# Four raw buffers, four weight slots and smaller groups in the first FFN pass of a hybrid attention and mLSTM layer

## The chip, the cores and the metric

The kernel runs on one core of a Trainium2 chip. The metric is the device time of one execution in microseconds (us). Five engines work side by side, each through its own instructions in order: TensorE (PE) multiplies 128-wide tiles into PSUM, VectorE (DVE) and ScalarE (ACT) do the elementwise work, GpSimd (POOL) a little more of it, and SyncE (SP) issues the DMAs. An instruction starts when those ahead of it on its engine have started and the results that it needs are there.

## What is computed

One layer of a flow-matching backbone: attention and an mLSTM scan side by side, joined by an output projection, then a SwiGLU feed-forward network (FFN), for 128 context tokens and 1024 latent tokens. What the change touches is the FFN and what runs beside its first part:

```python
def swiglu(h, w_gu, w_down):
    g, u = jnp.split(h @ w_gu, 2, axis=-1)
    return (jax.nn.silu(g) * u) @ w_down
...
    mix = jnp.concatenate([attn_o, hm], axis=-1) @ w_out
    x = x + g1 * mix
    h2 = rmsnorm(x, norm2_w) * (1 + sc2) + sh2
    x = x + g2 * swiglu(h2, w_gu, w_down)
```

D_MODEL is 1024, D_FF 2816, that is 22 pieces `f` of 128. All values are 32-bit floats.

## The kernel before

The nine token blocks of 128 are taken three at a time (CT = 384 tokens). The FFN goes over its weights twice: a first pass for the first three blocks, while the attention of the other six is still being finished, and a second pass for those six. The second pass (`weights6`, `pair6`, L1588 on) uses sums of quarter matrices, in 16-bit parts, with fewer products.

**First pass.** `gate_up` (L1476) takes one `f` after another: for the gate and the up half it loads 128 x 1024 weights and runs 24 matmuls (`products`, L1472 to L1474). Weights and activations are split in an upper part that TensorE takes at full rate and a lower part for the rest, so each product is three matmuls. `load_piece` (L157) makes the split: a DMA into a raw buffer (L173), a cast on ACT into the upper part `whi` (L174), a subtraction on DVE into the lower part `wlo` (L175, recorded as L145), and for `gate_up` a sum of magnitudes on ACT (L178, the tally, tile `jk`), from which the second pass takes its scale. Then tanh on ACT (L1490), two products on DVE (L1491, L1492, tile `tn`, which also free the PSUM banks), and the split of the result into `hl` (ACT L1495, POOL). `down` (L1499) multiplies a group of up to five `f` with 512 columns of the down weights (L1214 to L1216); each of its three results is scaled by the gate on DVE (L1203) and added to the residual (L1204).

**Buffers.** Each name in `raw_tags` and `piece_tags` is a pair of buffers. Before, one raw pair (two raw buffers) and five pairs for `whi` and `wlo` serve the first pass; a counter walks round them. The fifth pair, `iraw0`, becomes a second raw pair when the second pass begins.

**Groups.** The 22 `f` go in groups of 4, 4, 4, 5 and 5. The first three are woven with the attention of the other blocks: scores S on TensorE (L1128), maximum on DVE (L1130), exponential on ACT (L1131), upper part `ph` on ACT (L1134) and lower part `pl` on DVE (L1135), turned by DMA (L1137, L1138), times values on TensorE (`po`, L1152, L1153), rescaled by ACT L1155 and DVE L1157. The last two groups are woven with the output projection of the last three blocks (`attn_out`, L1250 to L1254) and with `features6`, which scales (ACT L1553), transposes (PE L124) and splits (L1561 to L1585) the inputs of the second pass.

**Joint of the passes.** After the last `down`, `weight_scale` (L1537) takes the largest tally, transposes it (L124), finds a power of two on one partition (DVE L200, L190 to L193, tile `pv`), and spreads it with a matmul (L204) and a copy (L205). ACT L1605 and DVE L1606 then scale and split the weights of `f` 0 (and their sums `S`, L1597 to L1600), and the second pass's matmuls (L1619 to L1621) begin.

**What sets the order.** The order of each engine's instructions is fixed when the kernel is built, by a scheduler that runs the written program through its own model of time; `weave` hands it pieces of two streams in turn. The hardware keeps that order.

Of the kernel before, what the change touches and what calls it, by code (L numbers as in the profile page):

```python
# [8 lines left out]
F32 = mybir.dt.float32  # L9
# [4 lines left out]
AF = mybir.ActivationFunctionType  # L14
# [19 lines left out]
CB = 3  # L34
NCH = NB // CB
CT = CB * P
GROUPS = [(0, 4), (4, 4), (8, 4), (12, 5), (17, 5)]
SIX = [(0, 4), (4, 4), (8, 4), (12, 4), (16, 3), (19, 3)]
T1, T2, T3, T4, B22, B11, B21 = range(7)
A11, A12, S3, S1, S2, S4, A22 = range(7)  # L40
# [2 lines left out]
NG = 3  # L43
# [6 lines left out]
def hybrid_step(ctx: ExitStack, tc: tile.TileContext, I: dict, O: dict):  # L50
    nc = tc.nc
    mm = nc.tensor.matmul
    act = nc.scalar.activation
# [12 lines left out]
    def weave(main, side, n_main, n_side):  # L66

        due = 0.0
        for units in main:
            due += n_side / n_main * (units or 1)  # L70
            while due >= 1.0:
                next(side, None)
                due -= 1.0

    def emit(gen):
        for _ in gen:
            pass

    def chain(*gens):
        for g in gens:  # L80
            for v in g:
                yield v
# [67 lines left out]
    raw_tags = ["iraw1"]  # L150
    piece_tags = ["wl", "ipair1", "ipair0", "wq", "iraw0"]
# [5 lines left out]
    def load_piece(srcs, shape, raw=None, own=None, tally=None):  # L157

        a, b = shape
        n = a * b  # L160

        def view(t):
            return t[:, :n].rearrange("p (a b) -> p a b", b=b)

        raw = raw_tile() if raw is None else raw
        if not own:
            loaded["n"] = (loaded["n"] + 1) % len(piece_tags)
            tag = piece_tags[loaded["n"]]
            at = homes.get(tag, wp)
            own = [at.tile([P, 1024], F32R, name=nm(t), tag=tag, bufs=2) for t in ("whi", "wlo")]  # L170
        hi, lo = own
        for part, ap_ in srcs:
            loaded["piece"] = dma(part(view(raw)), ap_).ins  # L173
        nc.scalar.copy(hi[:, :n], raw[:, :n])  # L174
        sub(lo[:, :n], raw[:, :n], hi[:, :n].bitcast(F32), "dve")  # L175
        if tally is not None:
            jk = ft.tile([P, D], BF16, name=nm("jk"), tag="t2", bufs=nt2[0])
            act(jk[:, :n], raw[:, :n], AF.Abs, accum_out=wsum[:, tally : tally + 1])  # L178
        return view(hi), view(lo)

    full_view = lambda v: v
# [1317 lines left out]
    def down(c, a, f0, nf, n):  # L1499
        g = gate_bc(1, c, n)  # L1500
        acts = a["act"]
        pieces = []
        for j in range(0, nf, 2):
            m = min(2, nf - j)
            rows = w_down[(f0 + j) * P : (f0 + j + m) * P, n * 512 : (n + 1) * 512].rearrange("(a p) n -> p a n", p=P)
            pieces.append(load_piece([(full_view, rows)], (m, 512)))
        yield from three_blocks(
            lambda k, i: (acts[k][0][:, i * P : (i + 1) * P], acts[k][1][:, i * P : (i + 1) * P]),
            pieces, nf, lambda i, ps: add_gated(a["x1"][i], ps, g(c * CB + i), n))
# [27 lines left out]
    def weight_scale():  # L1537

        dve.tensor_reduce(out=six[:, 7:8], in_=wsum, axis=AX.X, op=ALU.max)
        emit(power_scale(fp, ones, six[:, 7:8], six[:, 2:4]))  # L1540
        dve.tensor_tensor(out=six[:, 4:5], in0=six[:, 1:2], in1=six[:, 3:4], op=ALU.mult)
        dve.tensor_tensor(out=six[:, 6:7], in0=six[:, 4:5], in1=six[:, 4:5], op=ALU.mult)
        dve.tensor_scalar(out=six[:, 5:6], in0=six[:, 4:5], scalar1=0.5, scalar2=None, op0=ALU.mult)
# [44 lines left out]
    def weights6(f):  # L1588

        raws = []  # L1590
        for off in (0, D_FF):
            raw = raw_tile()
            dma(raw.rearrange("p (k n) -> p k n", k=KD), w_gu[f + (NF if off else 0)].rearrange("p (k n) -> p k n", k=KD))
            raws.append(raw)
        g, u = (raw.rearrange("p (a n) -> p a n", a=2) for raw in raws)
        S = sp.tile([P, 4, 512], F32, name=nm("S"), tag="S", bufs=1)
        dve.tensor_tensor(out=S[:, 1], in0=u[:, 0], in1=u[:, 1], op=ALU.add)  # L1597
        dve.tensor_tensor(out=S[:, 0], in0=u[:, 0], in1=g[:, 0], op=ALU.add)
        dve.tensor_tensor(out=S[:, 2], in0=S[:, 1], in1=g[:, 0], op=ALU.add)
        dve.tensor_tensor(out=S[:, 3], in0=S[:, 2], in1=g[:, 1], op=ALU.add)  # L1600
        ops = {}
        for names, v in (((A11, A12), g), ((S2, S4), S[:, 2:4]), ((S3, S1), S[:, 0:2]), ((A22,), u[:, 1:2])):
            n = len(names)
            t = a4p.tile([P, 2, 2, 512], F16, name=nm("A"), tag="A4", bufs=7)
            act(t[:, 0:n, 0], v, AF.Copy, scale=six[:, 2:3])  # L1605
            dve.scalar_tensor_tensor(out=t[:, 0:n, 1], in0=v, scalar=six[:, 2:3], in1=t[:, 0:n, 0], op0=ALU.mult, op1=ALU.subtract)  # L1606
            for j, name in enumerate(names):
                ops[name] = [t[:, j, part].rearrange("p (k n) -> p k n", k=4) for part in range(2)]
        return ops

    def pair6(f, Bt, acts):

        ops = weights6(f)
        a, b, c, d = (bank()[:, 0:CT] for _ in range(4))

        def product(n, ps, first):
            (wh, wl), bt = ops[PRODUCTS[n][0]], Bt[:, PRODUCTS[n][1]]
            for k in range(4):
                mm(ps, wh[:, k], bt[:, 0, k], start=first and k == 0, stop=False, skip_group_check=True)  # L1619
                mm(ps, wh[:, k], bt[:, 1, k], start=False, stop=False, skip_group_check=True)  # L1620
                mm(ps, wl[:, k], bt[:, 0, k], start=False, stop=k == 3, skip_group_check=True)  # L1621

        def u(tag, bufs=1):
            return up.tile([P, CT], F32, name=nm(tag), tag=tag, bufs=bufs)

        product(0, a, True)
        p1 = u("p1", 2)
        nc.scalar.copy(p1, a)
        yield
        product(1, b, True)  # L1630
        u2 = u("u2", 2)
        dve.tensor_tensor(out=u2, in0=b, in1=p1, op=ALU.subtract)
        yield
        product(2, d, True)
        yield
        product(3, c, True)
        u3 = u("u3")
        dve.tensor_tensor(out=u3, in0=c, in1=u2, op=ALU.add)
        c22 = u("c22")
        dve.tensor_tensor(out=c22, in0=u3, in1=d, op=ALU.subtract)  # L1640
        yield
        product(4, a, False)
        tn = up.tile([P, 2, CT], F32, name=nm("tn"), tag="tn", bufs=2)
        act(tn[:, 0], a, AF.Tanh, scale=six[:, 5:6])
        yield
        product(5, d, False)
        gb = u("gb")
        dve.tensor_tensor(out=gb, in0=d, in1=u2, op=ALU.subtract)
        act(tn[:, 1], gb, AF.Tanh, scale=six[:, 5:6])
        dve.scalar_tensor_tensor(out=tn[:, 1], in0=tn[:, 1], scalar=1.0, in1=c22, op0=ALU.add, op1=ALU.mult)  # L1650
        dve.tensor_tensor(out=tn[:, 1], in0=tn[:, 1], in1=gb, op=ALU.mult)
        yield
        product(6, c, False)
        c21 = u("c21")
        dve.tensor_tensor(out=c21, in0=c, in1=u2, op=ALU.add)
        dve.scalar_tensor_tensor(out=tn[:, 0], in0=tn[:, 0], scalar=1.0, in1=c21, op0=ALU.add, op1=ALU.mult)
        dve.tensor_tensor(out=tn[:, 0], in0=tn[:, 0], in1=a, op=ALU.mult)
        hl = new_hl(f)
        flat = tn.rearrange("p a n -> p (a n)")
        act(hl[:, 0], flat, AF.Copy, scale=six[:, 6:7])  # L1660
        dve.scalar_tensor_tensor(out=hl[:, 1], in0=flat, scalar=six[:, 6:7], in1=hl[:, 0].bitcast(F32), op0=ALU.mult, op1=ALU.subtract)
        acts.append(hl)
        yield
# [117 lines left out]
    cur, nxt = {}, {}  # L1781
    cur["x1"], nxt["x1"] = x1_first, new_x1(1)
    due = 0.0
    for _ in prefill(cur, nxt):
        due += 0.35
        while due >= 1.0:
            with tc.issue_after(cur["gate"]), tc.issue_after(loaded["gate"]), tc.issue_after(loaded["hm"]), tc.issue_after(loaded["pe"]):
                next(att, None)
            due -= 1.0

    hlp = es_f.enter_context(tc.tile_pool(name="hlp", bufs=1, reuse_waits="tile"))

    def groups(c, a, lst):
        for f0, nf in lst:
            yield from gate_up(a, f0, nf)
            yield from down(c, a, f0, nf, 0)
            yield from down(c, a, f0, nf, 1)
# [14 lines left out]
    with tc.issue_after(loaded["gate"]):  # L1812
        for _ in range(4):
# [10 lines left out]
    firsts = []  # L1824
    feats = chain(*[features6(nxt, 1, i, Bt, firsts) for i in range(CB)],
                  attn_out(far, o2, g_d[0, 1], lambda i: mixing(a4p, "A4", 7), o_d[CB:]), *[features6(far, 2, i, Bt, firsts) for i in range(CB)])
    main = groups(0, cur, GROUPS[NG:])
    weave(main, feats, 18 * sum(nf for _, nf in GROUPS[NG:]), 42)
    emit(feats)
    weight_scale()  # L1830
    es_f.close()
    es_ps.close()
    del psum["mm1"], psum["po"]
# [4 lines left out]
    nt2[0] = 4  # L1838
    ft = ctx.enter_context(tc.tile_pool(name="ft6", bufs=1, reuse_waits="tile"))
    fp = ctx.enter_context(tc.tile_pool(name="fp6", bufs=1, reuse_waits="tile"))  # L1840
    raw_tags.append(piece_tags.pop())
    x6 = nxt["x1"] + far["x1"]
    gs6 = row_pair(g_d[1, 1])
    done6 = finish(0, cur)
# [67 lines left out]
```

## Time and profile before

| | us |
|---|---|
| median of 3 runs (1538.3 to 1539.11) | 1538.46 |
| the profiled execution | 1538.01 |
| its span | 1536.2 |
| first pass, first L1472 to last down matmul | 651.97 to 1024.2 |
| first matmul of the second pass | 1028.40 |

Mean granted clock of TensorE 0.97. Times in the trace count from the start of the span; some 1.8 us of the execution lie outside it. A row of the timeline gives start, length, engine, line, operation, result and operands, and in brackets how long the engine stood idle before it and what ended that.

### The profile page before, as it was taken

To read this page: it belongs to the slowest core of one execution; us is meant where nothing else is said; L and a number is where in the kernel's file an instruction comes from. 1 tells how busy PE (TensorE), PEld (TensorE's weight loads), DVE (VectorE), ACT (ScalarE), POOL (GpSimd) and SP (SyncE) were. 2 spreads that over 40 slices of the span, in tenths; PEclk is the share of its full clock that TensorE was granted. 3 is DMA by queue.
4 is the path that set the end of the run, shared out by engine and by line. 5 is a ranking of instruction groups with operands and counts; after the bars stand their busy time and mean duration, and the time that the engine had idled before them with its cause. 6 is when DMAs were issued, how large, how long until landed. Compare 5 with 4: busy or idle time off the path is not lost.

```text
span 1536.2 us, 22786 instructions
## 1 busy us (share of the span) xinstructions
PE 1434.6 (93%) x8281; PEld 1071.1 (70%) x8281; DVE 1126.6 (73%) x2272; ACT 810.7 (53%) x1524; POOL 222.4 (14%) x310
## 2 busy tenths in 40 slices
PE   6889899899899889999999899989999999999995
PEld 3635567676677657888989787965766667676763
DVE  4978557685777778646787766879878696886857
ACT  4855476676766745552866752844334141523233
POOL 0122332132323344510001010000000000000000
PEclk9799999999999999999999999999999999999997
DMA  9475245565449756564778733444222040412112
GB/s 371 155 227 186 68 90 96 72 150 78 81 102 158 197 187 170 145 206 138 212 177 193 185 117 117 143 132 153 81 72 94 28 137 1 138 49 76 35 35 82
DMA packets 255318, 197.02 MB, mean 128 GB/s; under 512 B 167974, under 2 KB 209142, under 8 KB 255206
## 3 DMA queue, kind: packets, MB, share of 16 engines
q1 hardware_dynamic: 252638, 191.13, 45.9%
q10 hardware_dynamic: 2440, 4.05, 1.2%
q8 instruction: 65, 1.06, 0.3%
q0 software_dynamic: 128, 0.39, 0.1%
q14 instruction: 47, 0.39, 0.1%
HBM read 143.94 MB, written 13.26 MB: 102 GB/s over the span
## 4 chain that ended last, share of the span: by engine, by line
PE 53%; DVE 4%; DMA 4%; ACT 4%; issue 1%; POOL 1%; SPq 0%; ACTq 0%; POOLq 0%
PE mm L1621 7%; PE mm L1619 7%; PE mm L1620 7%; PE mm L1687 4%; PE mm L1688 4%; PE mm L1689 4%; PE mm L1472 3%; PE mm L1474 3%; PE mm L1473 3%; PE mm L1214 2%; PE mm L1216 2%; PE mm L1215 2%; PE mm L1250 2%; DMA raw<-in_w_gu_dram 2%; PE mm L1252 2%; PE mm L1254 1%
## 5 line engine op out<-in xcount | busy, mean ns | idle before, releaser
L1619 PE MATMUL mm<-Bt,A 128*128 128x384 f16 x616 | 200.2, 328 | 1.6 <-ACT A L1605 1.6
L1620 PE MATMUL mm<-Bt,A 128*128 128x384 f16 x616 | 201.6, 327 | 0.0
L1621 PE MATMUL mm<-Bt,A 128*128 128x384 f16 x616 | 197.2, 327 | 2.4 <-DVE A L1606 2.4
L174 ACT CAST whi<-raw 128x1024 fp32r<-128x1024 f32 (+1 forms) x102 | 103.3, 1014 | 132.5 <-DMA raw<-in_w_down_dram 49.0
L145 DVE TENSOR_TENSOR wlo<-raw,whi 128x1024 fp32r<-128x1024 f32 (+1 forms) x102 | 120.7, 1183 | 53.8 <-ACT whi L174 49.0
L1135 DVE SCALAR_TENSOR_TENSOR pl<-pr,st,ph 128x1152 f16<-128x1152 f32 (+1 forms) x72 | 95.7, 1329 | 48.8 <-ACT ph L1134 45.1
L1472 PE MATMUL mm<-aTh,whi 128*128 128x384 f32 x352 | 121.7, 346 | 8.8 <-ACT ol L1155 3.1
L1474 PE MATMUL mm<-aTh,wlo 128*128 128x384 f32 x352 | 120.9, 344 | 0.8 <-DVE wlo L145 0.8
L1473 PE MATMUL mm<-aTl,whi 128*128 128x384 f32 x352 | 120.9, 343 | 0.0
L1130 DVE TENSOR_REDUCE st<-S 128x1 f32<-128x1152 f32 (+1 forms) x72 | 88.9, 1235 | 21.7 <-PE S L1128 21.2
L1131 ACT ACTIVATE pr<-S,st 128x1152 f32<-128x1152 f32 (+1 forms) x72 | 81.5, 1132 | 40.2 <-DVE st L1130 39.7
L1134 ACT ACTIVATE ph<-pr,st 128x1152 f16<-128x1152 f32 (+1 forms) x72 | 84.0, 1167 | 32.4 <-DVE st L1133 11.7
L1128 PE MATMUL S<-kst,qT 128*128 128x384 f32 (+1 forms) x400 | 89.6, 357 | 7.1 <-ACT pr L1131 7.1
L525 PE MATMUL wi<-headw,hT 128*128 128x384 f16 x288 | 94.7, 329 | 1.6 <-ACT th L815 1.4
L526 PE MATMUL wi<-headw,hT 128*128 128x384 f16 x288 | 94.6, 328 | 0.0
L527 PE MATMUL wi<-headw,hT 128*128 128x384 f16 x288 | 94.5, 328 | 0.0
L1605 ACT ACTIVATE A<-S,six 128x1024 f16<-128x1024 f32 x44 | 49.9, 1146 | 80.8 <-PE mm L1621 58.0
L1619 PEld LDWEIGHTS <-A 128*128 128x128 f16 x616 | 60.3, 98 | 44.5 <-issue 3.8
L1621 PEld LDWEIGHTS <-A 128*128 128x128 f16 x616 | 60.4, 98 | 43.2 <-DVE A L1606 3.1
L1203 DVE TENSOR_TENSOR t<-mm,hmr 128x512 f32<-128x512 f32 x84 | 54.4, 684 | 48.3 <-PE mm L1689 33.3
L1620 PEld LDWEIGHTS <-A 128*128 128x128 f16 x616 | 60.4, 98 | 39.2 <-issue 0.5
L1128 PEld LDWEIGHTS S<-kst,qT 128*128 128x128 f32 x400 | 71.0, 194 | 10.7 <-ACT pr L1131 8.4
(456 smaller groups left out, 3694.3 us busy)
## 6 DMA issues: line engine op xcount, KB each, us to landing
raw<-in_w_gu_dram SPq DMA_DIRECT2D x88, 512.0 KB
raw<-in_w_down_dram SPq DMA_DIRECT2D x40, 512.0 KB
a<-in_w_ada_dram SPq DMA_DIRECT2D x24, 512.0 KB
iraw<-in_w_in_dram SPq DMA_DIRECT2D x32, 256.0 KB
x<-in_x_sample_dram SPq DMA_DIRECT2D x11, 512.0 KB
raw<-in_w_out_dram SPq DMA_DIRECT2D x10, 512.0 KB
aw<-in_w_ada_dram SPq DMA_DIRECT2D x8, 512.0 KB
aw<-in_w_ada_dram SPq DMA_DIRECT2D x16, 256.0 KB
```

The costliest lines, as they stand in the source:

```text
L145: (dve if eng == "dve" else pool).tensor_tensor(out=out, in0=full, in1=hi, op=ALU.subtract)
L174: nc.scalar.copy(hi[:, :n], raw[:, :n])
L525: mm(ps[:, :n], ah, wh[:, k % 2, c0 : c0 + n], start=(k == 0), stop=False)
L526: mm(ps[:, :n], ah, wl[:, k % 2, c0 : c0 + n], start=False, stop=False)
L1128: mm(S[:, n, 0:w], qT[:, h, :], kst[kv][:, t, c0 + n * w : c0 + (n + 1) * w], start=(t == 0), stop=(t == 1))
L1135: dve.scalar_tensor_tensor(out=plv, in0=prv, scalar=st[:, 3:4], in1=phv, op0=ALU.mult, op1=ALU.subtract)
L1472: mm(ps, wh[:, k, :], th[:, k, :], start=(k == 0), stop=False)
L1473: mm(ps, wh[:, k, :], tl[:, k, :], start=False, stop=False)
L1474: mm(ps, wl[:, k, :], th[:, k, :], start=False, stop=(k == KD - 1))
L1619: mm(ps, wh[:, k], bt[:, 0, k], start=first and k == 0, stop=False, skip_group_check=True)
L1620: mm(ps, wh[:, k], bt[:, 1, k], start=False, stop=False, skip_group_check=True)
L1621: mm(ps, wl[:, k], bt[:, 0, k], start=False, stop=k == 3, skip_group_check=True)
```

## The change

1. The second raw pair is joined before the first pass: four raw buffers and four weight slots there, instead of two and five.
2. The groups of the first pass are 4, 4, 4, 4, 3 and 3, as those of the second pass are. That is one more group: six more scaled additions (L1203 and L1204, twelve rows on DVE) and four more loads of gate rows. Matmuls, weight loads and casts keep their number.
3. The tally reads the upper part of the weights instead of the raw buffer. (A magnitude then lacks its low bits; it only serves to choose a power of two.)
4. The last group's second `down` is written behind `features6`; its first step, `weight_scale`, `weights6(0)`, and the rest of it follow one another, so that the second pass's first weights can be made ready behind the last down pieces.

```diff
-GROUPS = [(0, 4), (4, 4), (8, 4), (12, 5), (17, 5)]
+GROUPS = [(0, 4), (4, 4), (8, 4), (12, 4), (16, 3), (19, 3)]
...
-            act(jk[:, :n], raw[:, :n], AF.Abs, accum_out=wsum[:, tally : tally + 1])
+            act(jk[:, :n], hi[:, :n].bitcast(F32), AF.Abs, accum_out=wsum[:, tally : tally + 1])
...
-        ops = weights6(f)
+        ops = weights6(f) if f > 0 else first_ops
...
+    raw_tags.append(piece_tags.pop())
     hlp = es_f.enter_context(tc.tile_pool(name="hlp", bufs=1, reuse_waits="tile"))
...
-    main = groups(0, cur, GROUPS[NG:])
-    weave(main, feats, 18 * sum(nf for _, nf in GROUPS[NG:]), 42)
+    main = chain(groups(0, cur, GROUPS[NG:-1]), gate_up(cur, *GROUPS[-1]), down(0, cur, *GROUPS[-1], 0))
+    weave(main, feats, 18 * sum(nf for _, nf in GROUPS[NG:-1]) + 15 * GROUPS[-1][1], 42)
     emit(feats)
+    main = down(0, cur, *GROUPS[-1], 1)
+    next(main)
     weight_scale()
+    first_ops = weights6(0)
+    emit(main)
...
-    raw_tags.append(piece_tags.pop())
     x6 = nxt["x1"] + far["x1"]
```

How the instructions move, at three places. Names carry the numbers of the tiles.

**SP, before the first pass and at its beginning.** raw_1581 and raw_1585 are the gate and up weights of `f` 0, raw_1593 and raw_1597 those of `f` 1. Before, at 575.9 us and at the beginning of the pass:

```order
L173 DMA raw_1581_7888<-in_w_gu_dram 128x1024
L1234 DMA gl_1414_7100<-g_d_81 128x512
L1234 DMA gl_1415_7102<-g_d_81 128x512
L173 DMA raw_1585_7920<-in_w_gu_dram 128x1024
...
L1138 DMA_TRANSPOSE plT_1547_7710<-pl_1563_7778 128x9x128
L1192 DMA gx_1631_8196<-g_d_81 128x512
L1314 DMA x1_d2_90<-t2_1577_7877 128x512
L173 DMA raw_1593_7961<-in_w_gu_dram 128x1024
L173 DMA raw_1597_7993<-in_w_gu_dram 128x1024
```

And after:

```order
L173 DMA raw_1593_7961<-in_w_gu_dram 128x1024
L1234 DMA gl_1414_7100<-g_d_81 128x512
L1234 DMA gl_1415_7102<-g_d_81 128x512
L173 DMA raw_1597_7993<-in_w_gu_dram 128x1024
...
L1138 DMA_TRANSPOSE plT_1547_7710<-pl_1563_7778 128x9x128
L1188 DMA gl_1630_8194<-g_d_81 128x512
L1314 DMA x1_d2_90<-t2_1572_7835 128x512
L173 DMA raw_1581_7888<-in_w_gu_dram 128x1024
L173 DMA raw_1585_7920<-in_w_gu_dram 128x1024
L173 DMA raw_1624_8153<-in_w_gu_dram 128x1024
```

The loads of `f` 0 and of `f` 1 have changed places; TensorE still takes `f` 0 first.

**PE and ACT, at the transposes of the third token block.** t2_2183 (before) and t2_2189 (after) are the scaled inputs that L124 transposes; mm_2173 and mm_2183 are products of `gate_up`. Before, on PE and then on ACT:

```order
L1472 MATMUL mm_2173_10949<-aTh_1483_7374,whi_2179_10985 128x384
L124 MATMUL mm_2184_11021<-ident_91,t2_2183_11019 128x128 x4
L1473 MATMUL mm_2173_10949<-aTl_1484_7375,whi_2179_10985 128x384
...
L174 CAST whi_2179_10985<-raw_2178_10984 128x1024
L178 ACTIVATE jk_2181_10990,wsum_7083<-raw_2178_10984 128x1024
L1553 ACTIVATE t2_2183_11019<-x1_1710_8552,ry_2119_10626 128x512
```

And after, on PE and then on ACT:

```order
L1474 MATMUL mm_2183_10958<-aTh_1483_7374,wlo_2193_11007 128x384
L124 MATMUL mm_2190_10996<-ident_91,t2_2189_10994 128x128 x4
L124 MATMUL mm_2196_11039<-ident_91,t2_2195_11037 128x128 x4
L1472 MATMUL mm_2199_11055<-aTh_1483_7374,whi_2202_11058 128x384
...
L174 CAST whi_2219_11174<-raw_2218_11173 128x1024
L178 ACTIVATE jk_2187_10965,wsum_7083<-whi_2185_10960 128x1024
L1553 ACTIVATE t2_2189_10994<-x1_1710_8552,ry_2109_10581 128x512
L178 ACTIVATE jk_2194_11011,wsum_7083<-whi_2192_11006 128x1024
L1553 ACTIVATE t2_2195_11037<-x1_1710_8552,ry_2109_10581 128x512
```

The transposes stand behind the last matmul of a piece now, not within one, and ahead of their inputs on ACT stands the cast of whi_2219, which goes into the slot of whi_2192 and so waits for that same last matmul of mm_2183.

**DVE, at the end of the pass.** mm_2258 is the bank of the nine down matmuls that now stand ahead of L204 on PE; S_2252 are sums for the second pass. Before:

```order
L1203 TENSOR_TENSOR t2_2235_11287<-mm_2233_11253,gl_2219_11211 128x512
L200 TENSOR_REDUCE pv_2237_11293<-mm_2236_11291 1x1
L1204 TENSOR_TENSOR x1a_6529<-x1a_6529,t2_2235_11287 128x512
L190 TENSOR_SCALAR pv_2237_11293<-pv_2237_11293 1x1
L191 TENSOR_SCALAR pv_2237_11293<-pv_2237_11293 1x1
L192 TENSOR_SCALAR pv_2237_11293<-pv_2237_11293 1x1
L193 TENSOR_SCALAR pv_2237_11293<-pv_2237_11293 1x1
L205 COPY six_7082<-mm_2238_11299 128x2
```

And after, first some ten rows ahead, then from the transposed tally on:

```order
L1597 TENSOR_TENSOR S_2252_11309<-raw_2251_11307 128x512
...
L1491 SCALAR_TENSOR_TENSOR tn_2222_11205<-tn_2222_11205,mm_2213_11138 128x384
...
L200 TENSOR_REDUCE pv_2248_11293<-mm_2247_11291 1x1
L1204 TENSOR_TENSOR x1a_6529<-x1a_6529,t2_2236_11261 128x512
...
L1203 TENSOR_TENSOR t2_2260_11352<-mm_2258_11332,gl_2238_11267 128x512
L1204 TENSOR_TENSOR x1a_6529<-x1a_6529,t2_2257_11329 128x512
L191 TENSOR_SCALAR pv_2248_11293<-pv_2248_11293 1x1
L1204 TENSOR_TENSOR x1a_6529<-x1a_6529,t2_2260_11352 128x512
L192 TENSOR_SCALAR pv_2248_11293<-pv_2248_11293 1x1
L193 TENSOR_SCALAR pv_2248_11293<-pv_2248_11293 1x1
L205 COPY six_7082<-mm_2249_11299 128x2
```

The sums S stand ahead of the last products of `gate_up`, and the scale's small rows stand among scalings and additions.

## The prediction

> **What bounds the kernel now.** TensorE is busy for 93% of the span (the page's first line), so only stretches in which it stands still or runs slowly can give time back. The first view is busy time by stretch, over the first FFN pass (651.97 to 1024.2) and its edges: stretch in us, its length, then busy us of PE, PEld, DVE, ACT, POOL, the granted clock, DMA share and GB/s. The second lists what TensorE waited for from 650 to 1036: total us, times, longest.
>
> ```profile
> 650.00:672.00 22.00, 18.94 (x104) 17.72 (x103) 7.69 (x11) 10.66 (x18) 4.56 (x3) 0.92 0.76 195
> 672.00:858.00 186.00, 185.04 (x1009) 167.98 (x1008) 138.09 (x201) 113.49 (x162) 14.44 (x11) 1.00 0.68 179
> 858.00:895.00 37.00, 30.12 (x178) 28.28 (x178) 23.35 (x37) 27.45 (x44) 2.03 (x2) 0.95 0.63 170
> 895.00:966.00 71.00, 67.25 (x328) 58.88 (x326) 44.74 (x80) 30.98 (x49) 5.07 (x3) 0.98 0.41 129
> 966.00:1022.00 56.00, 56.00 (x303) 52.31 (x303) 43.20 (x62) 35.07 (x55) 5.96 (x5) 1.00 0.41 133
> 1022.00:1036.00 14.00, 7.99 (x35) 4.34 (x34) 11.45 (x31) 8.01 (x11) 0.00 (x0) 0.76 0.45 151
> ```
>
> ```profile
> PE mm L1472 <- ACT ol L1155: 3.1, 1, 3.1
> PE mm L1472 <- ACT whi L174: 3.1, 1, 3.1
> PE mm L1472 <- DVE tn L1492: 2.4, 1, 2.4
> PE mm L1621 <- DVE A L1606: 2.4, 1, 2.4
> PE mm L124 <- ACT t L1553: 2.2, 1, 2.2
> PE mm L204 <- DVE pv L193: 2.0, 1, 2.0
> PE mm L1619 <- ACT A L1605: 1.6, 1, 1.6
> PE po L1153 <- DMA plT<-pl: 1.1, 1, 1.1
> PE mm L1250 <- DVE t L1203: 0.9, 1, 0.9
> PE mm L1474 <- DVE wlo L145: 0.8, 1, 0.8
> ```
>
> These are single waits, 20 us in all. 672 to 858 and 966 to 1022 have next to none, so a change of the first pass can win at four places only. Waits also cost clock: where they are dense the granted clock falls (22 x 0.08 = 1.8 us of clock missing, 37 x 0.05 = 1.9, 14 x 0.24 = 3.4), and matmuls of one shape start 0.32 us apart instead of 0.18:
>
> ```profile
> 652.15 0.34 PE L1473 MATMUL mm<-aTl,whi 128*128 128x384 f32 x1
> 652.33 0.34 PE L1474 MATMUL mm<-aTh,wlo 128*128 128x384 f32 x1
> ...
> 963.76 0.52 PE L1473 MATMUL mm<-aTl,whi 128*128 128x384 f32 x1
> 964.08 0.52 PE L1474 MATMUL mm<-aTh,wlo 128*128 128x384 f32 x1
> ```
>
> So a wait of 2 us or more costs its length and about 1.6 us of slow clock behind it (the slow rows at 963 stand behind the 2.2 us wait of L124). The Trainium skill, "TensorE: Matmul & The Clock Gate", section "What's actually happening", has the array fall to half clock only after an idle window of about 3.4 us. By that rule only the new wait at the entry would be followed by a slow clock, and the sum below would be 6.1 us smaller (1.3 + 3 x 1.6). The trace differs (half clock behind 2.2 us), and I go by the trace.
>
> **The change, part by part.** Matmuls and weight bytes stay the same. Losses now: entry 3.1 + 1.6 = 4.7; 858 to 895, 6.9 + 1.7 = 8.6; 895 to 966, 3.75 + 1.6 = 5.3; 1022 to 1036, 6.0 + 2.2 (the part of the 3.4 in which it worked) = 8.2.
>
> Entry of the pass. With four raw buffers f 0's two loads fall on the newly joined pair, which still holds the last piece of the output projection; they wait for its last matmuls, and stand behind plT and three short DMAs on SP. Those of f 1 and one of f 3 go early in their place, but TensorE still starts with f 0.
>
> ```profile
> 651.06 1.08 PE L1254 MATMUL mm<-whi,mx 128*128 128x512 f32 x4
> 653.96 2.00 SPq L1138 DMA_TRANSPOSE plT<-pl  x1
> 658.46 1.37 SPq L173 DMA_DIRECT2D raw<-in_w_gu_dram  x2
> 663.80 1.04 ACT L174 CAST whi<-raw 128x1024 fp32r<-128x1024 f32 x1 [3.81 <-DMA raw<-in_w_gu_dram]
> 666.17 0.33 SPq L173 DMA_DIRECT2D raw<-in_w_gu_dram  x1
> 669.44 1.05 ACT L174 CAST whi<-raw 128x1024 fp32r<-128x1024 f32 x1 [0.66 <-DMA raw<-in_w_gu_dram]
> ```
>
> plT can start at about 651.9 and takes 2.0, the short DMAs about 1.3: loads leave at 655.2. A pair took 5.3 us to its cast (658.46 to 663.80), a single load 3.3 (666.17 to 669.44); I take 5, since these are a pair. With the cast (1.05) TensorE starts f 0 at 661.2 instead of 652.0. Of the 9.2 us, 2.0 are filled by 18 po matmuls that moved ahead; the third matmul then waits 1.0 more for the low half; slow clock 1.6. Loss 9.8, **5.1 more** than now (1.3 to 6.2, by the two load times and with or without the clock).
>
> Middle (858 to 895). The casts come earlier, tn L1491 stands ahead of the softmax rows on DVE, and the 3.1 and 2.4 us waits go (the first L1472 after 869 reads the bank that L1491 frees; the page names another). Late next is the last head's softmax:
>
> ```profile
> L1130 DVE TENSOR_REDUCE st<-S 128x1 f32<-128x1152 f32 (+1 forms) x72 | 88.9, 1235 | 21.7 <-PE S L1128 21.2
> L1131 ACT ACTIVATE pr<-S,st 128x1152 f32<-128x1152 f32 (+1 forms) x72 | 81.5, 1132 | 40.2 <-DVE st L1130 39.7
> L1134 ACT ACTIVATE ph<-pr,st 128x1152 f16<-128x1152 f32 (+1 forms) x72 | 84.0, 1167 | 32.4 <-DVE st L1133 11.7 <-issue 8.9 <-DMA phT<-ph 4.3
> 876.89 1.85 SPq L1137 DMA_TRANSPOSE phT<-ph  x1
> 880.85 0.28 PE L1152 MATMUL po<-phT,vs 128*128 128x256 f16 x1 [0.20 <-DMA phT<-ph]
> ```
>
> From its last S matmul to po it needs 1.24 + 1.13 + 1.17 + 3.96 (876.89 to 880.85) = 7.5, and about 2.2 in the queues of ACT and DVE; TensorE has 27 matmuls at 0.18 and 16 of po, 6.5 us. It waits 3.2, then 0.8 for plT, and 1.4 for phT of the head before; with 1.3 of clock 6.7 instead of 8.6: **1.9 gained** (0 to 5). The 0.8 us wait of L1474 goes too: **0.8 gained** (0 to 0.8).
>
> The transposes of features6. Four weight slots instead of five make the cast of a new piece wait for TensorE's last matmul of the piece four before. ACT works in order, and the L1553 rows that TensorE's next instruction (L124) reads now stand right behind such a cast. ACT's durations:
>
> ```profile
> 959.59 0.49 ACT L1490 ACTIVATE tn<-mm 128x384 f32<-128x384 f32 x1 [3.53 <-PE mm L1474]
> 960.32 1.05 ACT L178 ACTIVATE jk<-raw 128x1024 bf16<-128x1024 f32 x1
> 961.36 0.71 ACT L1553 ACTIVATE t<-x,ry 128x512 f32<-128x512 f32 x1
> 982.26 1.05 ACT L174 CAST whi<-raw 128x1024 fp32r<-128x1024 f32 x1
> ```
>
> For the third token block TensorE ends mm_2183, and ACT only then does cast, tally and L1553: 1.05 + 1.05 + 0.7 = 2.8 idle; then tally and L1553 again less four transposes, 1.05 + 0.7 - 0.7 = 1.0. With the clock **5.4 lost** (3.0 to 6.5) in a stretch that has no wait now. For the first block tanh, cast, L1553 and then tally, L1553 give 2.1 + 1.0 + 1.6 = 4.7, and 1.0 goes at the joins of the output projection, 5.7 against 5.3: **0.4 lost** (2 lost to 1 gained).
>
> Sums S of pass 2. L1597 now stands on DVE ahead of tn_2222, and its load follows the last low half of a raw buffer: 3.3 to 5 us in which DVE holds back L1491 and L1492. TensorE has work for most of it: **1.0 lost** (0 to 3).
>
> End of the pass. Nine down matmuls go ahead of the scale's matmul L204 and nine behind.
>
> ```profile
> 1024.45 0.68 DVE L1203 TENSOR_TENSOR t<-mm,gl 128x512 f32<-128x512 f32 x1
> 1027.19 1.15 ACT L1605 ACTIVATE A<-raw,six 128x1024 f16<-128x1024 f32 x1
> 1030.33 1.28 DVE L1606 SCALAR_TENSOR_TENSOR A<-raw,six,A 128x1024 f16<-128x1024 f32 x1
> ```
>
> But DVE's rows of the scale stand among ten adds of 0.6 (L1203, L1204). The first nine wait for three L1203 (1.1 idle); the ten adds and five small rows, 6.9, against 2.9 of matmuls and that 1.1 leave 2.9; behind L204 come 0.8 + 1.15 + 1.28 against nine matmuls and two of pass 2, 2.4: 0.9. The clock (1.6), and p1 behind three L1435 of 1.0, about 1.0. 7.5 instead of 8.2: **0.7 gained** (1.5 lost to 4 gained).
>
> At nothing: twelve more adds (12 x 0.6 = 7 us of DVE, beside matmuls; uncovered only at the end, counted there), four gate DMAs, and the tally, which keeps its length. It no longer holds the raw buffer, but the low half's subtraction does.
>
> Sum: 5.1 - 1.9 - 0.8 + 5.4 + 0.4 + 1.0 - 0.7 = **8.5 slower**: 1538.0 (profiled run; span 1536.2) becomes 1546.5, and from the median 1538.46, 0.45 above it, 1546.9.
>
> **The rivals.** *Weights ahead everywhere (faster).* If from 672 on the pass ran like 966 to 1022, with no wait, it would win 1.0 + 8.6 + 5.3 = 14.9 and 0.7 at the end, less 5.1: 1528. It decides at the casts: if ACT has them done before TensorE's last matmul of the slot, L1553 is never late. For it speaks that 49 us of ACT's waits are for raw loads; against it that they cost TensorE little, and that the order sets cast before L1553. The Trainium skill, "Perfetto Trace Analysis", section "Optimization Strategy", reads repeated gaps as too few buffers; by that rule this rival wins. The gaps quoted above are single, with different releasers. *Cancelled.* If the clock stays up behind the new waits other than the entry's (1.3 + 3 x 1.6 = 6.1: each is cut in two by four transposes or nine matmuls, which may keep it up), and the pair of loads lands in 3.3 us as the single one did (1.7), 1546.9 - 6.1 - 1.7 = 1539.1. Against it stands the slow clock behind 2.2 us. The rule of the Trainium skill on the clock, above, leads here too. *The entry and the end at their worst:* 1546.9 + 1.1 + 1.1 + 2.2 + 2.0 + 3 = 1556.
>
> **How the numbers follow.** Forecast 0.62 (1541.5 to 1553), cancel 0.15, weights ahead 0.15, worst 0.08. Two runs differ by about 0.2% without any change, 3.1 us, so 1535.4 to 1541.5 is the same. Slower 0.62 + 0.08 = 0.70, same 0.15, faster 0.15. The range, 1534 to 1553, leaves out most of the faster rival and of the worst.
>
> **What would show it.** Right: an idle of 6 us or more before the first L1472 of the pass, released by whi L174; L124 waiting twice for L1553 in the stretch before the end; a wait of L204 for pv of 2 us or more; 858 to 895 still with idle released by phT or plT. Wrong: f 0 starting right behind the output projection, L124 without waits, or L204 covered by the nine matmuls.

## The result, and the profile after

| | before | after |
|---|---|---|
| median, us (lowest to highest, 5 runs each) | 1538.46 (1536.93 to 1541.89) | 1551.47 (1548.4 to 1552.94) |
| the profiled execution; its span | 1538.01; 1536.2 | 1551.47; 1549.7 |
| mean granted clock | 0.97 | 0.97 |

The ratio, worked out from all runs, is 1.0072, 95% interval 1.0053 to 1.0091: **11.1 us slower** (8.2 to 14.0); the two medians alone differ by 13.0. The forecast was 1546.9 (1534 to 1553), slower; the median lies 4.6 us above it, inside the range. The first view of after is busy time by stretch, as in the prediction: stretch in us, its length, busy us of PE, PEld, DVE, ACT, POOL, granted clock, DMA share and GB/s. The second is what TensorE waited for from 645 to 1050: total, times, longest.

```profile
650.00:672.00 22.00, 16.36 (x81) 13.79 (x79) 7.37 (x10) 11.04 (x17) 2.56 (x2) 0.84 0.75 231
672.00:858.00 186.00, 185.78 (x1018) 169.29 (x1017) 133.09 (x195) 110.74 (x158) 14.49 (x12) 1.00 0.68 178
858.00:895.00 37.00, 33.55 (x199) 30.96 (x197) 24.87 (x42) 28.82 (x46) 2.01 (x2) 0.95 0.67 173
895.00:966.00 71.00, 64.70 (x313) 56.79 (x313) 50.01 (x84) 36.34 (x59) 4.11 (x3) 0.96 0.43 137
966.00:1022.00 56.00, 51.52 (x270) 48.22 (x269) 44.01 (x67) 31.13 (x48) 4.37 (x4) 0.96 0.36 113
```

```profile
PE mm L124 <- ACT t L1553: 7.0, 4, 2.8
PE mm L204 <- DVE pv L193: 4.3, 1, 4.3
PE po L1153 <- DMA plT<-pl: 3.2, 2, 2.7
PE po L1152 <- DMA phT<-ph: 2.9, 2, 2.3
PE mm L1214 <- DVE t L1203: 2.8, 2, 1.8
PE mm L1472 <- ACT whi L174: 1.7, 1, 1.7
```

The stretch 966 to 1022, which had no wait before, now has 4.5 us of idle and a clock of 0.96; 895 to 966 loses 6.3 us of idle instead of 3.75; 858 to 895 wins (3.45 idle for 6.9). L124 waits four times for L1553, where it waited once for 2.2 us. The rows of the timeline (start, length, engine, line, operation, operands, in brackets the idle time before and its releaser) put the new waits at the entry, at the transposes of the first and third block, and at the scale:

```profile
656.51 0.29 PE L1153 MATMUL po<-plT,vs 128*128 128x256 f16 x1 [2.71 <-DMA plT<-pl]
661.93 0.44 PE L1472 MATMUL mm<-aTh,whi 128*128 128x384 f32 x1 [1.74 <-ACT whi L174]
...
961.22 1.11 PE L124 MATMUL mm<-ident,t 128*128 128x128 f32 x4 [0.99 <-ACT t L1553]
...
1002.57 0.66 PE L124 MATMUL mm<-ident,t 128*128 128x128 f32 x4 [2.80 <-ACT t L1553]
1004.22 0.66 PE L124 MATMUL mm<-ident,t 128*128 128x128 f32 x4 [1.00 <-ACT t L1553]
...
1039.30 0.58 PE L204 MATMUL mm<-pv,ones 1*128 1x2 f32 x2 [4.34 <-DVE pv L193]
```

**How the loss is counted.** At full clock TensorE's matmuls start at fixed steps, read from the traces: 0.1755 us for L1472 to L1474, 0.228 for L1214 to L1216 and L1250 to L1254, 0.163 for L1619 to L1621, 0.109 for po, 0.103 for L124. For each kernel I took the time since one matmul that all have (the first L1250 of the last output projection ahead of the pass) and subtracted the steps of all matmuls issued since. What is left is idle and slow clock together. It leaves out what varied ahead of the pass. The table gives the loss in us by stretches of this work, each column ending where its head says (0 to 24 the entry; 206 to 230 the middle; 279 to 303 the transposes of the first block; 303 to 339 those of the others; 339 to 363 the end of the pass; then pass 2), for all kernels of this study, and behind it the timed ratio to the kernel before with its interval (for the change, from its own comparison; for the others from 6 to 12 runs against 18 to 27 of the kernel before). Each row of losses is one traced execution.

```
                 0-24 -206 -230 -279 -303 -339 -363 -448   sum  ratio
before            5.0  2.1  9.3  2.9  4.0 -0.2  8.6  4.8  36.5
after             9.6  1.0  5.5  4.3  6.4  6.7  9.3  5.9  48.8  1.0072 [1.0053, 1.0091]
e1_shift          1.7  1.0  5.9  4.3  5.2  6.7  8.3  4.8  37.9  1.0024 [1.0008, 1.0040]
e2_join_late      0.2  2.7  9.4  5.0  7.1  6.5  8.7  4.8  44.3  1.0047 [1.0031, 1.0062]
e3_join_only     10.2  1.0  6.2  1.1  3.5  0.3  6.8  4.7  33.7  0.9974 [0.9955, 0.9993]
e4_groups_only    2.0  5.6  9.2  8.3  2.5  5.0  9.6  4.8  46.9  1.0063 [1.0041, 1.0085]
e5_join_shift     0.7  1.3  6.8  0.8  4.9 -0.1  6.8  4.8  25.9  0.9941 [0.9916, 0.9965]
e6_five_groups    1.6  1.0  6.0  2.9  1.7  0.4  4.6  5.4  23.5  0.9923 [0.9895, 0.9951]
e7_place          9.5  1.0  5.4  3.7  8.8  1.6  9.4  4.8  44.1  1.0050 [1.0032, 1.0069]
e8_own_junk      10.1  1.2  2.3  6.3  5.4  2.7  8.5  4.8  41.3  1.0028 [1.0015, 1.0042]
e9_five_one_four  0.9  1.1  5.9  2.6 12.8  1.3  2.5  5.5  32.6  0.9979 [0.9964, 0.9995]
e10_five_junk     0.9  1.2  2.3  2.7  1.6  1.2  5.6  5.6  21.2  0.9893 [0.9868, 0.9918]
e11_five_tally    0.9  1.1  5.7  1.2  6.8  0.2  6.9  4.8  27.5  0.9945 [0.9924, 0.9965]
e12_scale_early   1.9  1.0  5.4  2.6  1.6  0.4  1.7  6.1  20.8  0.9899 [0.9875, 0.9924]
```

Where the order of the matmuls differs, the same amount of work is not the same matmul, so a stretch is good to about 1 us; whether the clock falls behind a wait can move one by 1.4 us more (e3 and e5 at 279 to 303; last section). The sums agree with the ratios: the change loses 12.3 us more than before by the count and 11.1 by the ratio, and the other kernels lie within 2.5 us.

### The profile page after: what moved, and what is told of

Same layout as the page of the kernel before. It is cut to its first block, busy times and chain, and to the rows that moved or that the text cites. A ratio compares the mean times of both kernels' runs of the same rounds, so it can differ in the third digit from the quotient of the medians.

```text
span 1549.7 us, 22841 instructions
## 1 busy us (share of the span) xinstructions
PE 1436.4 (93%) x8281; PEld 1070.8 (69%) x8281; DVE 1134.0 (73%) x2284; ACT 810.9 (52%) x1524; POOL 219.0 (14%) x310
## 4 chain that ended last, share of the span: by engine, by line
PE 55%; DVE 5%; DMA 3%; ACT 2%; issue 1%; POOL 1%; SPq 0%; ACTq 0%; DVEq 0%; POOLq 0%
PE mm L1619 6%; PE mm L1621 6%; PE mm L1620 6%; PE mm L1472 4%; PE mm L1474 4%; PE mm L1473 4%; PE mm L1687 4%; PE mm L1688 4%; PE mm L1689 4%; PE mm L1250 2%; PE mm L1214 2%; PE mm L1215 2%; PE mm L1216 2%; PE mm L1252 2%; PE mm L1254 1%; PE S L1128 1%
## 5 line engine op out<-in xcount | busy, mean ns | idle before, releaser
L1619 PE MATMUL mm<-Bt,A 128*128 128x384 f16 x616 | 199.7, 327 | 0.7 <-DVE u L1638 0.7
L1621 PE MATMUL mm<-Bt,A 128*128 128x384 f16 x616 | 198.0, 327 | 0.0
L174 ACT CAST whi<-raw 128x1024 fp32r<-128x1024 f32 x102 | 103.0, 1014 | 131.0 <-PE mm L1215 37.9
L145 DVE TENSOR_TENSOR wlo<-raw,whi 128x1024 fp32r<-128x1024 f32 x102 | 121.9, 1196 | 43.2 <-ACT whi L174 39.2
L1472 PE MATMUL mm<-aTh,whi 128*128 128x384 f32 x352 | 122.2, 347 | 2.3 <-ACT whi L174 1.7
L1474 PE MATMUL mm<-aTh,wlo 128*128 128x384 f32 x352 | 120.7, 343 | 0.6 <-DVE wlo L145 0.6
L1134 ACT ACTIVATE ph<-pr,st 128x1152 f16<-128x1152 f32 (+1 forms) x72 | 84.1, 1168 | 33.2 <-DVE st L1133 11.4
L1619 PEld LDWEIGHTS <-A 128*128 128x128 f16 x616 | 60.4, 98 | 43.0 <-issue 3.6
L1621 PEld LDWEIGHTS <-A 128*128 128x128 f16 x616 | 60.4, 98 | 40.0 <-issue 0.3
L1203 DVE TENSOR_TENSOR t<-mm,hmr 128x512 f32<-128x512 f32 x84 | 55.0, 685 | 45.2 <-PE mm L1689 33.6
L1128 PEld LDWEIGHTS S<-kst,qT 128*128 128x128 f32 x400 | 70.2, 192 | 12.9 <-ACT pr L1131 10.6
```

The source lines that it names most:

```text
L145: (dve if eng == "dve" else pool).tensor_tensor(out=out, in0=full, in1=hi, op=ALU.subtract)
L1128: mm(S[:, n, 0:w], qT[:, h, :], kst[kv][:, t, c0 + n * w : c0 + (n + 1) * w], start=(t == 0), stop=(t == 1))
L1472: mm(ps, wh[:, k, :], th[:, k, :], start=(k == 0), stop=False)
L1474: mm(ps, wl[:, k, :], th[:, k, :], start=False, stop=(k == KD - 1))
```

## The experiments

**Which part loses.** My theory at first was the prediction's: the early join of the raw pair costs at the entry and at the transposes, where casts wait for one of four weight slots. The rival: the smaller groups cost. Four kernels.

e1_shift is the changed kernel with the buffer counter set back:

```diff
     raw_tags.append(piece_tags.pop())
+    loaded["raw"] = -1
```

> The changed kernel, but the count of the raw buffers is set back at the join, so that the two loads of f 0 fall on the old pair and those of f 1 on the new one. Theory (f 0 waits for the buffer that the output projection still holds): f 0 starts right behind the output projection again, the wait shrinks to one of about 3 us at f 1, the entry loses 5 us instead of 9.7, 1547 in all. Rival (the loads are late because they stand on SP behind the transposes plT and the short DMAs, whatever buffer they use): TensorE still waits 6 us or more of work before f 0, 1551.

e2_join_late is the changed kernel with the join where it was:

```diff
-    raw_tags.append(piece_tags.pop())
     hlp = es_f.enter_context(tc.tile_pool(name="hlp", bufs=1, reuse_waits="tile"))
...
+    raw_tags.append(piece_tags.pop())
     x6 = nxt["x1"] + far["x1"]
```

> The changed kernel with the fourth raw pair taken from the weight slots only at the start of pass 2, as before (five slots and two raw buffers in pass 1). Theory (four slots make the casts stand ahead of L1553, and the new pair delays f 0): the entry gives back 4.5 us, the waits of L124 for L1553 (4.6 us idle with clock, third block) go, the middle loses its 3.8 again; 1541 to 1543. Rival (what is lost behind 895 comes from the groups of at most four, which put one more down phase with its adds and waits among the features): only the entry comes back and the middle is lost, so 1550 to 1551, with L124 still waiting for L1553 before the last group.

e3_join_only moves this one line the other way, in the kernel before.

> The kernel before with nothing but the early join: four raw buffers and four weight slots in pass 1, groups, tally and first weights as before. Theory: entry +4.5, middle -3.8 and -1.3 around it, the waits of L124 for L1553 in the features of the second chunk +5 to +7; 1543 to 1546. Rival (groups): entry +4.5 and middle -5.1 cancel, no new wait of L124; 1538.

e4_groups_only is the kernel before with the change's `GROUPS`.

> The kernel before with nothing but groups of at most four (six groups instead of five). Theory: one more down phase costs its waits only, +1 to +3; 1540 to 1541, L124 without waits of 2 us in the second chunk. Rival (groups are the cause of what is lost behind 895): +8 or more, 1547, with L124 waiting for L1553.

**Measured.** e1 settles the entry: with f 0 on the old pair its loss falls from 9.6 to 1.7 us (I had expected 5), and 0.5% of the time comes back. The buffer delayed f 0, not the place of the loads on SP. For the rest the rival won. The groups alone cost 0.63% (9.7 us, 6.3 to 13.1); the join alone **gains** 0.26% (4.0 us, 1.1 to 6.9), although it loses 5.2 us at the entry. The parts do not simply add: 9.7 less 4.0 is 5.7, and the change loses 11.1. Some of the difference lies at the entry: without the join, e2 and e4 lose only 0.2 and 2.0 there, where the kernel before loses 5.0, and the join's delay of f 0 undoes that. What else makes it up no run separates. The waits of TensorE in e3 from 645 to 1050 show f 0 late and L124 with a single wait, with four weight slots:

```profile
PE mm L1472 <- ACT whi L174: 3.5, 1, 3.5
PE po L1153 <- DMA plT<-pl: 2.9, 2, 2.3
PE po L1152 <- ACT whi L174: 2.2, 1, 2.2
PE mm L204 <- DVE pv L193: 1.9, 1, 1.9
PE mm L1472 <- DVE F L1563: 1.7, 1, 1.7
...
PE mm L124 <- ACT t L1553: 1.3, 1, 1.3
```

and those of e2, with five slots, show the four waits of L124 again. Here are ACT's rows ahead of the third block's transposes, first of the change, then of e2:

```profile
999.81 1.04 ACT L174 CAST whi<-raw 128x1024 fp32r<-128x1024 f32 x1 [2.68 <-PE mm L1474]
1000.76 1.05 ACT L178 ACTIVATE jk<-whi 128x1024 bf16<-128x1024 f32 x1
...
1001.81 0.71 ACT L1553 ACTIVATE t<-x,ry 128x512 f32<-128x512 f32 x1
```

```profile
999.61 1.04 ACT L174 CAST whi<-raw 128x1024 fp32r<-128x1024 f32 x1 [3.37 <-DMA raw<-in_w_gu_dram]
1000.56 1.05 ACT L178 ACTIVATE jk<-whi 128x1024 bf16<-128x1024 f32 x1
...
1001.61 0.71 ACT L1553 ACTIVATE t<-x,ry 128x512 f32<-128x512 f32 x1
```

Both have the cast, the tally and L1553 in this order, and the cast begins at the same time: in the change because TensorE has left the slot, in e2 because the load is there. With either number of slots L1553 comes 2.5 to 2.8 us too late for TensorE. What both share is the groups.

e4 without any other edit does not wait at L124 but all over the second half; its waits from 885 on:

```profile
PE mm L204 <- DVE pv L193: 4.3, 1, 4.3
PE mm L1472 <- DVE F L1563: 3.3, 1, 3.3
PE mm L1472 <- DVE tn L1492: 2.8, 1, 2.8
PE mm L1619 <- ACT A L1605: 2.5, 2, 1.9
PE mm L1472 <- DVE ry L141: 1.7, 1, 1.7
PE mm L1250 <- DVE t L1203: 1.3, 1, 1.3
```

Most releasers are on DVE. My own expectation for e4 (1 to 3 us) missed; the rival's size came true, but not its sign, L124 waiting for L1553.

**How the groups lose.** With groups of 4, 3 and 3 a down phase ends 48 matmuls ahead of the third block's transposes. New theory A: L1553 and the tally write into the three `t` buffers that the adds of that down phase still hold, so they come behind L1204. Theory B: the prediction's. e5 and e6 test the sum of it all: the best use of the join, without and with the other edits but without the groups. e5_join_shift is e3 with e1's line.

> The kernel before with the early join and the count of the raw buffers set back at it (the loads of f 0 on the old pair); groups, tally and first weights as before. Theory (the join gains once f 0 is not delayed, the groups alone lose): the first two matmul groups of the pass lose about 2 us instead of the 10 of the join alone, the rest as in the join alone; against the kernel before a ratio of 0.992 to 0.995. Rival (the loss at the entry was already hidden in the timed runs, which put the join alone at 0.997): 0.997, no better than the join alone.

e6_five_groups is e1 with the `GROUPS` of before.

> The changed kernel with the raw count set back at the join and the groups of before (two of five at the end); so it differs from e1_shift in the groups alone. Theory (groups): 8 to 10 us less than e1_shift, whose ratio was 1.0024, so 0.996 to 0.998; no wait of L124 for L1553 over 1.5 us. Rival (the tally and the first weights share the loss, or the groups cost only without the join): within 3 us of e1_shift, 1.001 to 1.003.

e7_place is the changed kernel with 44 for 42:

```diff
-    weave(main, feats, 18 * sum(nf for _, nf in GROUPS[NG:-1]) + 15 * GROUPS[-1][1], 42)
+    weave(main, feats, 18 * sum(nf for _, nf in GROUPS[NG:-1]) + 15 * GROUPS[-1][1], 44)
```

> The changed kernel with one number of the weave changed, 44 for 42 units of side work, so that the transposes of the third token block no longer stand as eight in a row 48 matmuls behind a down phase; groups and buffers as in the change. Theory A (place: L1553 comes late where it stands behind the adds L1204 of a down phase, whose t buffers it needs, with a tally before it): the waits of L124 for L1553 shrink from 7.0 us to 3 or less, 4 to 7 us faster than the changed kernel, a ratio of 1.003 to 1.005. Theory B (slots, as predicted: L1553 stands behind casts that wait for one of four slots): the waits stay near 7 us, 1.007.

e8_own_junk is the changed kernel with

```diff
-            jk = ft.tile([P, D], BF16, name=nm("jk"), tag="t2", bufs=nt2[0])
-            act(jk[:, :n], hi[:, :n].bitcast(F32), AF.Abs, accum_out=wsum[:, tally : tally + 1])
+            jk = ft.tile([P, D], mybir.dt.float8e4, name=nm("jk"), tag="jk", bufs=1)
+            act(jk[:, :n], hi[:, :n].bitcast(F32), AF.Abs, accum_out=wsum[:, tally : tally + 1], saturate=False)
```

> The changed kernel, but what the tally L178 writes and nobody reads goes to a buffer of its own (one byte an element, for want of room) instead of one of the three t buffers that L1203 and L1553 use. TensorE's order around the transposes stays. Theory A (t buffers: tally and L1553 wait for L1204): the longest wait of L124 for L1553 falls from 2.8 to 1 us or less, the four together to 2 to 3 us, 4 to 6 us faster than the changed kernel, 1.003 to 1.005. Theory B (casts that wait for a slot): tally and L1553 stay behind the casts, 2.8 us as before, 1.007.

**Measured.** e5 is 0.6% faster than before, as expected, and e6 0.8%, more than expected. e6 differs from e1 in the `GROUPS` line alone (from which the pace of the last weave also follows): 0.9923 against 1.0024, 15.5 us. By the table they come from 279 to 303 (5.2 to 1.7), 303 to 339 (6.7 to 0.4) and the end (8.3 to 4.6). So the groups are the loss, with the join (e1, e6) as without it (before, e4).

By time e8 is 6.8 us better than the change (1.0028), a little more than theory A expected, and it bears theory A out at the third block: 303 to 339 falls from 6.7 to 2.7 us. ACT's rows there, in which L1553 now stands ahead of the cast that waits for the slot:

```profile
997.36 1.05 ACT L178 ACTIVATE jk<-whi 128x1024 fp8e4<-128x1024 f32 x1
...
998.40 0.72 ACT L1553 ACTIVATE t<-x,ry 128x512 f32<-128x512 f32 x1
1000.27 1.04 ACT L174 CAST whi<-raw 128x1024 fp32r<-128x1024 f32 x1 [1.15 <-PE mm L1473]
...
1001.57 0.71 ACT L1553 ACTIVATE t<-x,ry 128x512 f32<-128x512 f32 x1
```

The first L1553 now starts where the first add ends (998.30), and the first of L124's two waits is gone. The second L1553 still stands behind the cast, and 1.5 us of wait are left. In the change itself the two reasons end within 0.7 us of each other: the adds at 1000.05, the cast, which delays the tally to 1000.76, a little later. Only e8 parts them. But the longest wait of L124 did not fall to 1 us as I expected: at the first block it rose to 3.4. There L1553 waits for the norm `ry` on DVE, which begins with the last add of the output projection. First DVE's two rows of the change, the add and the end of the norm, then ACT's row of e8:

```profile
951.50 0.68 DVE L1204 TENSOR_TENSOR x<-x,t 128x512 f32<-128x512 f32 x1
...
958.11 0.16 DVE L141 SCALAR_TENSOR_TENSOR ry<-rt,ry 128x3 f32<-128x3 f32 x1
```

```profile
961.60 1.95 ACT L1553 ACTIVATE t<-x,ry 128x512 f32<-128x512 f32 x3 [0.26 <-DVE ry L141]
```

From the add to the end of the norm 6.8 us pass. Between the last matmul of the output projection and these transposes the change has 48 matmuls of gate and up (48 x 0.1755 = 8.4 us); the kernel before has 45 of down and 24 of gate and up (45 x 0.228 + 24 x 0.1755 = 14.5 us). The groups took this cover away. In the change itself the norm ends at 958.27 and L1553 starts at 958.80, behind a tanh and a cast, so by these rows I estimate that the norm explains 1.7 of the 2.2 us that L124 waits there; no run takes the norm alone out. I had not expected e8's gain in the middle (5.5 to 2.3): with the tallies elsewhere on ACT, the last head's upper part L1134 starts 3.3 us earlier in e8 (second row) than in the change (first row), although e8 came to the pass 2.0 us later, and TensorE no longer waits for phT there.

```profile
880.11 1.26 ACT L1134 ACTIVATE ph<-pr,st 128x1152 f16<-128x1152 f32 x1 [0.52 <-ACT pr L1131]
```

```profile
876.85 1.25 ACT L1134 ACTIVATE ph<-pr,st 128x1152 f16<-128x1152 f32 x1
```

e7 moved the wait rather than removing it: 303 to 339 falls from 6.7 to 1.6, and the first block's wait grows to 5.0 us, so L124 still waits 6.4 us, which is near what theory B expected. Its interval (1.0032 to 1.0069) reaches from theory A's range nearly to theory B's 1.007; by time it decides nothing.

**Number or place, and what is left to win.** e9_five_one_four is e1 with another cut of the same number of groups:

```diff
-GROUPS = [(0, 4), (4, 4), (8, 4), (12, 4), (16, 3), (19, 3)]
+GROUPS = [(0, 4), (4, 4), (8, 4), (12, 5), (17, 1), (18, 4)]
```

> e1_shift with the last ten f cut into groups of 5, 1 and 4 in place of 4, 3 and 3: the number of groups is the change's, but the first down phase behind the features stands where groups of five put it, and no transposes stand right behind a down phase. Theory (place: 4, 3, 3 put the output projection, the transposes and the down phases so that TensorE comes to the transposes before the norm and the adds are done): within 4 us of e6_five_groups, 0.993 to 0.996. Rival (number: each group more costs its adds, gates and small pieces wherever it stands): as e1_shift, 1.000 to 1.003.

e10_five_junk is e6 with e8's edit.

> e6_five_groups, and what the tally writes gets a buffer of its own, as in e8_own_junk. Theory (the t buffers hold L1553 back behind the adds): the one wait of L124 for L1553 left in e6 (1.4 us) goes, with its neighbours 1 to 3 us; 0.990 to 0.992. Rival (with groups of five the t buffers are free in time): no change, 0.992 to 0.993.

e11_five_tally is e5 with the tally from the high half.

> e5_join_shift and the tally from the high half: e6_five_groups without the early first weights. Theory (as in the prediction, the tally gives nothing): as e5_join_shift, 0.993 to 0.995, and the early first weights then make the difference to e6 (0.9923), if there is one. Rival (raw buffers that come free a tally earlier bring loads and casts forward): 0.992 or less, as e6.

e12_scale_early is e6 with

```diff
     emit(feats)
+    weight_scale()
     main = down(0, cur, *GROUPS[-1], 1)
     next(main)
-    weight_scale()
     first_ops = weights6(0)
```

> e6_five_groups with the scale of the weights worked out one step earlier, ahead of the last down phase's second half instead of behind its first nine matmuls: the scale's matmul L204 then stands behind 33 matmuls where it stood behind 2. Theory (L204 waits for rows that DVE works off between adds, and more matmuls ahead of it cover them): the wait of 2.4 us for pv falls below 0.5, 2 to 4 us less than e6, 0.990 to 0.991. Rival (DVE is the limit: sums S and A come no earlier, the wait moves to the first matmuls of pass 2): 0.992 to 0.993.

**Measured.** e9 fell between the two expectations (0.9979). By the table it is within 2.1 us of e6 up to 279 and from 303 on, and loses 11 us more from 279 to 303, where L124 waits 2.7 us and this row stands: TensorE has nothing to do while the only `hl` of the group of one is made.

```profile
973.32 0.79 PE L1214 MATMUL mm<-whi,hl 128*128 128x512 f32 x1 [4.34 <-ACT hl L1495]
```

So six groups need not cost what 4, 3, 3 costs, which speaks for the place; but every cut brings waits of its own, and a six-group kernel without them was not found. e10 and e12 came out as fast as expected or faster: **0.9893 and 0.9899**, 16.5 (12.6 to 20.3) and 15.5 us (11.7 to 19.2) faster than the kernel before. Against e6 their intervals overlap; by the count they gain 2.3 and 2.7 us. In e12 the stretch 339 to 363 falls from 4.6 to 1.7, and L204 waits no more. Its four largest waits from 645 to 1050 are:

```profile
PE po L1152 <- DMA phT<-ph: 2.4, 1, 2.4
PE mm L1214 <- DVE t L1203: 1.9, 2, 1.1
PE mm L124 <- ACT t L1553: 1.4, 1, 1.4
PE mm L1472 <- DVE tn L1491: 0.9, 2, 0.6
```

e10's gain is not at L124, as I expected, which still waits 1.4: the table has it in the middle (6.0 to 2.3), as in e8. e11 equals e5 (0.9945 and 0.9941): no gain of the tally from the high half shows with four raw buffers. From e11 to e6 the early first weights gain 0.2% by the medians of the ratios, with overlapping intervals, and 4.0 us by the count. e10's and e12's edits were not run together.

## Why the prediction was right, and where it was not

By its own terms, forecast and then measured from the table (after less before):

- **Entry**: +5.1, measured +4.6 (a loss of 9.6 where 9.8 was forecast). Right in mechanism, by e1 and e3 (10.2 with the join alone), and f 0 starts 9.1 us behind the output projection for the 9.2 forecast. But the idle came in pieces (0.55 and 2.71 ahead of po, 1.74 ahead of the first L1472, 0.64 ahead of L1474), not as the 6 us in one piece that was to be the sign, and it is 5.6 us where 8.2 were forecast; slow clock is 4.0 where 1.6 were. That the two errors cancel is luck.
- **The wait of L1474** (24 to 206): -0.8, measured -1.1.
- **Middle**: -1.9, measured -3.8. Right in kind: the casts come earlier, and phT is late next, for 2.3 us. e3 has it (6.2), e2 without the join does not (9.4). The term was too small by half: the waits are 3.5 us (0.60, 2.34 and 0.52) for the 5.4 forecast, and the wait for phT of the head before is not there.
- **First block and joins**: +0.4, measured +3.8 (230 to 303: 10.7 against 6.9). The two waits of L124 are as forecast, 2.19 and 0.99 us for 2.1 and 1.0. Too small were the joins of the output projection, 3.1 us of waits (0.96 of L1250, 1.83 of L1214 for t, 0.32 of L1250) for the 1.0 forecast, and the slow clock behind L124. The norm, which the matmuls of a down phase covered before, is not in the step.
- **Third block**: +5.4, measured +6.9, and 2.8 and 1.0 us idle to the tenth as forecast. **This step failed in its reason.** "Four weight slots instead of five make the cast of a new piece wait" is true of the change's trace, yet with four slots and the old groups (e3) the stretch loses 0.3, and with five slots and the new groups (e2) 6.5. The row of cast, tally and L1553 was read rightly from the order; it stands where it does because of the groups.
- **Sums S of pass 2**: +1.0, measured nothing. DVE did stand 3.54 us for their load (to 1020.03), as forecast, but TensorE has no wait over 0.1 us from 1004.22 to 1032.63. The +1.1 of the column of pass 2 comes later: L1619 waits 0.51 and 0.22 us for `u` (1072 and 1086), which no term names.
- **End**: -0.7, measured +0.7. L204 waited 4.3 us instead of the forecast 2.9; the waits for A and p1 that were to follow are gone. For 1.9 of the 4.3 us (0.24 and 1.64) DVE itself waits for gate rows from DMA, which stand ahead of the scale's small rows and which the term left out:

```profile
1037.18 0.69 DVE L1203 TENSOR_TENSOR t<-mm,gl 128x512 f32<-128x512 f32 x1 [1.64 <-DMA gl<-g_d]
```

  In e1 this wait is 0.86 and that of L204 3.3. Less the gate rows both are 2.4, near the forecast. (In the prediction's figure for the loss before, the part of the 3.4 us of slow clock in which TensorE worked, 8.0 of 14 us, is 1.9 and not 2.2.)

The sum was +8.5, the count says +12.3. The step that failed is the paragraph "At nothing": it priced the groups as twelve adds beside matmuls, 7 us of DVE, and their price measured alone is 9.7 us on the path (15.5 from e6 to e1, with the join), because they change what stands between the output projection, the transposes and the end. That the groups are the cause is shown; how the 9.7 us split among the norm, the `t` buffers and the end is only in part (e8, and the rows above). The join, to which the prediction gave +8.2 (entry, middle, L1474, both transposes' terms), gains 4.0 alone. So the total was near by luck: two prices, that of the join and that of the groups, were wrong in opposite directions.

The faster rival was nearer than its 0.15 as to mechanism: "weights ahead everywhere" less the entry. The Trainium skill, "Perfetto Trace Analysis", section "Optimization Strategy", which takes repeated gaps as a possible sign of too few buffers, leads there. e5 fits it as far as it goes: two more raw buffers, with one pair of weight slots less and f 0 not delayed, are worth 0.6% (9.1 us, 5.4 to 12.9), though the gaps of the kernel before were single ones. The rival of a clock that stays up did not come true: behind the 2.8 us wait the matmuls step by 0.32 us. But 1.6 us of slow clock behind every wait of 2 us or more is no rule either; the kernel before itself has a wait of 3.14 us without any (below).

## What to carry to other kernels

An edit that only regroups a loop is not priced by the instructions it adds: look at what it puts between a producer and the matmul that reads it, since the cover there was part of the old order. Where buffers are joined to a ring, look which of them the next load gets: here one line that set the counter back was worth 7.4 us (1.0072 to 1.0024), more than the 4.6 us that the delay added at the entry. And test every edit alone before believing the sum, even when the sum fits.

## What the runs showed of the hardware

- **The clock behind short waits.** Behind the change's waits of 2.80 and 1.00 us matmuls of one shape step by 0.32 us (half clock):

```profile
1004.97 0.52 PE L1473 MATMUL mm<-aTl,whi 128*128 128x384 f32 x1
1005.29 0.52 PE L1474 MATMUL mm<-aTh,wlo 128*128 128x384 f32 x1
```

  Behind a wait of 3.14 us in the kernel before they keep the step of full clock, 0.17:

```profile
872.09 0.41 PE L1472 MATMUL mm<-aTh,whi 128*128 128x384 f32 x1 [3.14 <-ACT ol L1155]
872.34 0.33 PE L1473 MATMUL mm<-aTl,whi 128*128 128x384 f32 x1
872.51 0.33 PE L1474 MATMUL mm<-aTh,wlo 128*128 128x384 f32 x1
```

  And the same two waits ahead of the same matmuls (1.25 us before L124, then 1.7 before L1472) left the clock up in e3 (first two rows) and were followed by half clock in e5 (last two); the granted clock of the 3.3 us behind them (966.2 to 969.5) is 1.00 and 0.53:

```profile
966.65 0.34 PE L1474 MATMUL mm<-aTh,wlo 128*128 128x384 f32 x1
966.83 0.34 PE L1472 MATMUL mm<-aTh,whi 128*128 128x384 f32 x1
```

```profile
966.97 0.53 PE L1474 MATMUL mm<-aTh,wlo 128*128 128x384 f32 x1
967.29 0.53 PE L1472 MATMUL mm<-aTh,whi 128*128 128x384 f32 x1
```

  The Trainium skill, "TensorE: Matmul & The Clock Gate", section "What's actually happening", has half clock only after about 3.4 us of idleness. These traces differ: 2.8 us in one piece, cut from the next by four transposes, was enough, and in the kernel before a single wait of 2.2 us. The length of a wait alone does not decide it in these runs; what does was not measured.

- **The time ahead of the pass varies.** The common matmul was reached between 646.3 us (before) and 659.1 us (e5) from the start of the span. The seven kernels whose counter is set back lie at 650.1 to 659.1, the seven others at 646.3 to 650.3. Part of that is the DVE order ahead of the pass, in which the counter changes the place of a low half; part was there by 490 us, where TensorE's order is the same in all. Single executions of one kernel spread too (e1: 1540.4 to 1549.8); that this is the reason is not shown, since one execution of each is traced. It is why the parts above are judged by the count and by intervals.
